# A hybrid decoder block: attention sinks as one more key column, and fewer vector operations around it

## The chip, the cores and the metric

The kernel runs on one core of a Trainium2 chip. The metric is device time in microseconds (us), from three runs: 1900.37, 1901.00 and 1901.44 us, median 1901.0. One execution was profiled as well. It took 1900.13 us, of which 1898.4 us lie between the first and the last instruction (the span).

The engines named below are PE (matrix products; PEld is its weight load), DVE (vector operations), ACT (activations and copies), POOL (masks and part of the DMA issues) and SP (the other DMA issues).

## The reference, cut to what matters

One layer over 2048 positions of width 1024, in float32: a normalized input is projected into a convolution branch, an attention branch and gates; both branches are gated, projected, merged and projected once more. The change lies in the attention, which has 16 query heads, 4 key heads, head size 64, blocks of 128 positions and a window of 128 keys. Each head has a learned sink, a score without a key: it takes part in the maximum and in the denominator, and in nothing else.

```python
qb = q.reshape(b, nb, BLOCK, N_KV_HEADS, g, HEAD_DIM)          # q, k are RMS-normalized per head
scores = jnp.einsum('bnqhgd,bnkhd->bnhgqk', qb, kb) * HEAD_DIM ** -0.5
scores = jnp.where(valid, scores, NEG_INF)                      # 0 <= q_pos - k_pos < 128
m = jnp.maximum(jnp.max(scores, axis=-1, keepdims=True), sink)
p = jnp.exp(scores - m)
p = p / (jnp.sum(p, axis=-1, keepdims=True) + jnp.exp(sink - m))
out = jnp.einsum('bnhgqk,bnkhd->bnqhgd', p, vb)
```

## The kernel before

**Products.** The sequence is worked in two tiles of 1024 positions. Every float32 operand is held as a high and a low part, and a product is done as high x high, low x high and high x low. A 1024-wide projection is cut into units of 256 output columns (`sunit`), and a unit is computed with seven block products instead of eight, in the manner of Strassen: products 1 and 2 use weight blocks as loaded, the others use sums of blocks. One product is 12 matmuls with 512 moving columns each. The units follow each other on PE without a break: keys, values, queries, convolution (`cv`, `b`), gates (`ga`, `gb`), `z`, `za`, then the output projections `yb`, `ya` and `o`.

**The clock of the program.** `run` counts products: each product is one tick. `put(n, f)` files a step for tick n, and the steps of a tick are written out after its product, in the order in which they were filed. Five engines get their instructions in this written order and each works its own queue strictly in order, so a step that must wait holds up all that stands behind it on its engine. `Woven` (`vec`) carries a list of small vector steps; each vector operation that goes through it takes one more step from that list along, and each tick ends with up to four of them.

**Weight sums.** For a unit, `sums` files four vector operations over the raw weights `raw[k, h]`, each 128x512: one addition, then `raw[0,0] = raw[0,1] - raw[0,0]`, then `raw[1,1] -= raw[0,0]` and `raw[1,0] -= raw[0,0]`. ACT then casts pairs of blocks to the high part, and DVE subtracts to get the low part.

**Attention.** It is woven between the products of `cv` to `z`: 32 blocks in each tile (4 key heads x 8 blocks), 64 in all, each with 4 query heads; `STEPS_0` and `STEPS_1` say at which tick a block's scores stand. The steps of a block whose scores stand at tick n are:

- n-5: load of the queries (`q2`), queries and keys (`kq`) and the keys' low parts (`kz`, two buffers `lows`);
- n: `att_scores`. Six matmuls on PE into one PSUM tile of two banks, of which there is a single buffer (`ps_s`, tile `s`): for each half h of the positions one matmul with the low parts of the keys (384 moving columns, for two heads c), then two with 192 columns (one for each head c). Each head has 256 columns in `s`, of which 192 are used. Then on DVE a masked copy, a maximum over 128 columns, and three operations on 128x4 values: the maximum times the query's scale `rq`, the smaller of its negative and minus the sink, and sink minus maximum;
- n+1: `att_exp`. On ACT one exponential of 128x4 for the sink, then for each head an exponential over 128 columns, which also gives the row sum;
- n+2: `att_norm` and `att_flip`. On DVE the row sum plus the sink's exponential, a reciprocal, the product with `p`, and a transposition;
- n+4 to n+15: two turns through memory, masks on POOL (`xh`, `yp`, `xl`), six matmuls with the values (`po`), and the sum into `o`.

`rq` holds the query scales of a head group, made on DVE well ahead of the first block that uses it.

## Time and profile before

| | before |
|---|---|
| median of 3 runs | 1901.0 us (1900.37 to 1901.44) |
| the profiled execution | 1900.13 us, span 1898.4 us |
| PE busy | 1888.9 us, 8670 matmuls |
| DVE busy | 1547.3 us, 2620 instructions |
| ACT busy | 986.6 us, 1967 instructions |
| POOL busy | 590.5 us |
| DVE busy between 1100 and 1150 us (attention stage) | 45.82 of 50 us |

Busy time is the time in which an engine has an instruction in work. The ends of matmuls are modelled and overlap, so whether PE stands still is read from the starts of its matmuls: a group of `x12` matmuls is one product, and its length divided by 12 is the spacing of the starts. In a line of the timeline, the numbers are start and duration in us; a bracket at the end names idle time before the instruction and what ended it.

### The profile page before, as it was taken

Reading aid. Unit: us, or ns where it says so; the run is one execution under the profiler, and the core shown is the slowest. Engines: PE = TensorE matmul, PEld = TensorE weight load, DVE = VectorE, ACT = ScalarE, POOL = GpSimd, SP = SyncE. Lnnn points to the kernel's source line nnn. Section 1 sums busy time; section 2 is a strip of 40 time slices with the busy share of each in tenths; the row PEclk is TensorE's granted clock in tenths of the full one; section 3 lists DMA queues with packets and bytes.
Section 4 is the critical chain, followed back from the end, with each engine's and each line's share of the span. In section 5 each row is a group of like instructions: output and inputs, shape, how many; then the busy total and the mean of one; then the engine's idle time right before and its main releaser. Section 6 shows DMA issues by size and latency. Waiting matters only on the chain.

```text
span 1898.4 us, 27426 instructions
## 1 busy us (share of the span) xinstructions
PE 1888.9 (100%) x8670; PEld 1572.3 (83%) x8670; DVE 1547.3 (82%) x2620; ACT 986.6 (52%) x1967; POOL 590.5 (31%) x846
## 2 busy tenths in 40 slices
PE   9999999999999999999999999999999999999999
PEld 7888888888888888888888888888888888888887
DVE  7988898898888767669799899888888777787754
ACT  7665455456666443434565545556666434444321
POOL 2073335335655000011462344445556000121000
PEclk9999999999999999999999999999999999999999
DMA  8286555558777857894584655567788887779653
GB/s 294 80 239 178 166 159 171 172 183 248 240 237 230 301 195 247 281 279 113 170 229 118 193 165 152 168 200 234 235 247 270 300 280 267 274 193 269 212 176 111
DMA packets 222497, 402.22 MB, mean 212 GB/s; under 512 B 30032, under 2 KB 104784, under 8 KB 212880
## 3 DMA queue, kind: packets, MB, share of 16 engines
q1 hardware_dynamic: 188224, 313.10, 50.4%
q0 software_dynamic: 30528, 78.94, 16.0%
q10 hardware_dynamic: 3600, 8.42, 1.3%
q8 instruction: 69, 1.13, 0.2%
q14 instruction: 76, 0.62, 0.1%
HBM read 271.09 MB, written 129.25 MB: 211 GB/s over the span
## 4 chain that ended last, share of the span: by engine, by line
PE 89%; DVE 5%; DMA 2%; ACT 2%; issue 1%; SPq 0%; POOL 0%; DVEq 0%; ACTq 0%; POOLq 0%
PE Y L640 33%; PE Xcv L640 4%; PE Vcv L640 4%; PE ya L1468 4%; PE Vq L640 2%; PE Xq L640 2%; PE Xyb L640 2%; PE Vyb L640 2%; PE Vo L640 2%; PE Xo L640 2%; PE Vza L640 2%; PE Xza L640 2%; PE po L1330 2%; PE Xgb L640 2%; PE Vgb L640 2%; PE Xga L640 2%
## 5 line engine op out<-in xcount | busy, mean ns | idle before, releaser
L1292 POOL DMA_DIRECT2D x<-fd x256 | 139.6, 552 | 128.8 <-DMA fd<-f 55.6
L1265 ACT ACTIVATE p<-s,st,rq 128x128 f32<-128x128 f32 x256 | 113.0, 450 | 0.1
L1313 POOL TENSOR_SCALAR_AFFINE_SELECT xh<-xh 64x512 fp32r<-64x512 f32 x64 | 59.3, 927 | 152.7 <-DVE xl L278 103.7
L1285 POOL DMA_DIRECT2D fd<-f x64 | 36.9, 577 | 209.4 <-DVE f L278 173.4
L1551 POOL DMA_DIRECT2D mt<-tha x16 | 13.8, 862 | 255.0 <-DVE tha L278 233.4
L640 PE MATMUL Xcv<-oph,wcv_ah 128*128 128x512 f32 x256 | 79.2, 390 | 0.0
L1313 POOL TENSOR_SCALAR_AFFINE_SELECT xl<-xl 64x512 fp32r<-64x512 f32 x64 | 66.2, 1034 | 4.4
L1313 POOL TENSOR_SCALAR_AFFINE_SELECT yp<-xl 64x512 fp32r<-64x512 f32 x64 | 58.2, 909 | 3.1
L1313 POOL TENSOR_SCALAR_AFFINE_SELECT yp<-yp 64x512 fp32r<-64x512 f32 x64 | 57.4, 898 | 4.2
L278 DVE SCALAR_TENSOR_TENSOR y<-u,cols,y 128x512 f32<-128x512 f32 x64 | 53.3, 834 | 3.8 <-ACT y L1379 2.7
L278 DVE TENSOR_TENSOR o<-po,o 64x256 f32<-64x256 f32 x128 | 53.4, 417 | 2.7 <-ACT o L1342 1.7
L640 PEld LDWEIGHTS Xcv<-oph,wcv_ah 128*128 128x128 f32 x256 | 47.6, 188 | 9.6
L278 DVE TENSOR_TENSOR p<-p,st 128x512 f32<-128x512 f32 x64 | 50.5, 790 | 3.3
L469 ACT CAST wcv_sh<-wcv_raw 128x1024 fp32r<-128x1024 f32 x16 | 16.8, 1051 | 69.7 <-DVE wcv_raw L278 69.7
L1265 ACT ACTIVATION_READ_ACCUMULATOR p<-s,st,rq 128x1 f32 x256 | 50.7, 198 | 0.0
L1342 ACT COPY o<-po 64x256 f32<-64x256 f32 x128 | 47.1, 368 | 6.2 <-DMA wpd_yb<-wph_yb 3.0
L1070 POOL DMA_DIRECT2D q2d<-q_h x64 | 44.2, 690 | 18.1 <-ACT q_h L1065 9.2
L640 PE MATMUL Xcv<-oph,wcv_al 128*128 128x512 f32 x128 | 49.8, 389 | 0.0
L2040 POOL DMA_DIRECT2D oc<-ocd x12 | 6.5, 543 | 136.0 <-DMA wyb_sh<-wpd_yb 119.7
L1070 POOL DMA_DIRECT2D q2d<-q_l x64 | 44.1, 689 | 13.7 <-DMA q2d<-q_h 5.0
L278 DVE TENSOR_TENSOR wcv_raw<-wcv_raw 128x512 f32<-128x512 f32 x64 | 47.3, 758 | 1.1
L278 DVE STREAM_TRANSPOSE f<-p 128x512 f32<-128x512 f32 x64 | 45.5, 711 | 2.9 <-DVE p L278 0.2
(713 smaller groups left out, 6457.9 us busy)
## 6 DMA issues: line engine op xcount, KB each, us to landing
gd<-th SPq DMA_DIRECT2D x64, 256.0 KB, 2.7
wcv_raw<-in_w_units SPq DMA_DIRECT2D x16, 1024.0 KB, 5.4
q<-q2d SPq DMA_DIRECT2D x64, 256.0 KB, 5.4
v<-vd SPq DMA_DIRECT2D x128, 128.0 KB, 3.5
fd<-f POOLq DMA_DIRECT2D x64, 256.0 KB, 4.4
x<-fd POOLq DMA_DIRECT2D x256, 64.0 KB, 3.2
th<-gd SPq DMA_DIRECT2D x48, 256.0 KB, 4.9
wga_raw<-in_w_units SPq DMA_DIRECT2D x8, 1024.0 KB, 5.3
```

Source lines behind the costliest of these rows:

```text
L278: r = f(*args, **kw)
L469: return (lambda: nc.scalar.copy(hi, src), lambda: vec.tensor_tensor(out=lo, in0=src, in1=hi.bitcast(F32), op=ALU.subtract))
L640: nc.tensor.matmul(ps, lhsT=w[:, j, :], rhs=b[:, m, :], start=start and j == 0 and i == 0, stop=j == KP - 1 and i == 2, skip_group_check=n ...
L1070: nc.gpsimd.dma_start(q2d[t][j][half, q * 2 * HB : (q + 1) * 2 * HB, i, e, :], src[HALVES[e]].bitcast(F32).rearrange("p (b x) -> p b x", x ...
L1265: nc.scalar.activation(out=p[:, i, :], in_=sg[:, i, HD : 3 * HD], func=AF.Exp, bias=st[:, 1, i : i + 1], scale=rv[:, i // 2, i % 2 : i % 2 ...
L1285: nc.gpsimd.dma_start(fd, f)
L1292: nc.gpsimd.dma_start(x[QUADS[k]], src[k])
L1313: nc.gpsimd.affine_select(out=d4, in_=s4, pattern=[[0, 2], [-32 * sg, 2], [0, G], [-sg, 32]], compare_op=ALU.is_gt if prev else ALU.is_ge, ...
L1330: nc.tensor.matmul(po[:, cs], lhsT=v2[:, kind + h, :], rhs=xx[:, :, h * HD : (h + 1) * HD], start=n == h == 0, stop=n == 2 and h == 1)
L1342: nc.scalar.copy(ov, pov[oth, :, e])
L1468: nc.tensor.matmul(ps, lhsT=w[:, j, cs], rhs=o[:, m, :], start=n == 0 and i == 0, stop=n == KC - 1 and i == 2)
L1551: nc.gpsimd.dma_start(mt[t][k, :, hs(q)], m, accum_op=ALU.add)
```

## The change

**The sink becomes a column.** For each head group, right after `rq` is made, DVE computes sink divided by `rq` for all its blocks (`keep_query`: a reciprocal and a product of 128x32, eight times in the kernel). Two ticks ahead of a block's scores a new step, `att_bank`, takes the tile `s` and has ACT copy the four quotients into column 192 of each head (128x4). Maximum, exponential and row sum then run over 129 columns instead of 128, so that the sink takes part in them. The 128x4 operations "times `rq`", "sink minus maximum" and "row sum plus sink" on DVE go, and so does the exponential of the sink on ACT. `p` has rows of 129 now, and the tiles of its pool are 2064 bytes long instead of 2048.

**Order of the score matmuls.** Within a half, the two matmuls of 192 columns come first, and the one of 384 columns comes last and adds to them.

**Weight sums.** The last two of the four subtractions in `sums` become one of 128x1024. `small` tiles have 10 buffers instead of 12, the tile `st` has 4 of its own.

```diff
+    def keep_query(t, j, rq):
+        rqs[t, j] = rq
+        sr = sinks_of[t, j] = consts.tile(
+            [P, 2, HB, 2, 2], F32, tag="sr_", bufs=4, name=f"sinks{t}_{j}")
+        s4 = sr.rearrange("p q b h c -> p (q b) (h c)")
+        vec.reciprocal(out=s4, in_=rq.rearrange("p q b h c -> p (q b) (h c)"))
+        mul(s4, s4, sink_r[:, j].rearrange("p h c -> p (h c)").unsqueeze(1).to_broadcast([P, NB, G]))
...
+    def att_bank(t, j, b):
+        sp = ps_s.tile([P, 2, 2, 2 * P], F32, tag="s", name=f"s{t}_{j}_{b}")
+        nc.scalar.copy(sp[:, :, :, 3 * HD : 3 * HD + 1], sinks_of[t, j][:, b // HB, b % HB].unsqueeze(3))
+        return sp
...
-            nc.tensor.matmul(
-                sp[:, h, :, skip : 3 * HD], lhsT=kq[:, 1, h * P : (h + 1) * P], rhs=kz[:, :, keys],
-                start=True, stop=False)
             for c in range(2):
                 nc.tensor.matmul(
                     sp[:, h, c, skip : 3 * HD], lhsT=q2[:, h, c, :], rhs=kq[:, 0, keys],
-                    start=False, stop=c == 1)
+                    start=c == 0, stop=False)
+            nc.tensor.matmul(
+                sp[:, h, :, skip : 3 * HD], lhsT=kq[:, 1, h * P : (h + 1) * P], rhs=kz[:, :, keys],
+                start=False, stop=True)
...
-        vec.tensor_reduce(out=st[:, 0], in_=sg[:, :, HD : 3 * HD], axis=AX.X, op=ALU.max)
-        mul(st[:, 5].rearrange("p (h c) -> p h c", c=2), st[:, 0].rearrange("p (h c) -> p h c", c=2), rv)
+        vec.tensor_reduce(out=st[:, 0], in_=sg[:, :, HD : 3 * HD + 1], axis=AX.X, op=ALU.max)
         vec.scalar_tensor_tensor(
-            out=st[:, 1], in0=st[:, 5], scalar=-1.0, in1=nsink_r[:, j].rearrange("p h c -> p (h c)"),
-            op0=ALU.mult, op1=ALU.min)
-        add(st[:, 2], sink_r[:, j].rearrange("p h c -> p (h c)"), st[:, 1])
+            out=st[:, 1], in0=st[:, 0], scalar=-1.0, in1=rv.rearrange("p h c -> p (h c)"),
+            op0=ALU.mult, op1=ALU.mult)
...
-        nc.scalar.activation(out=st[:, 3], in_=st[:, 2], func=AF.Exp)
-        p = slot([P, G, P], F32, f"p{t}_{j}_{b}")
+        p = slot([P, G, P + 1], F32, f"p{t}_{j}_{b}")
...
-        add(st[:, 5], st[:, 4], st[:, 3])
-        vec.reciprocal(out=st[:, 0], in_=st[:, 5])
+        vec.reciprocal(out=st[:, 0], in_=st[:, 2])
...
-                        lambda: sub(raw[:, 1, 1], raw[:, 1, 1], raw[:, 0, 0]),
-                        lambda: sub(raw[:, 1, 0], raw[:, 1, 0], raw[:, 0, 0])))
+                        lambda: sub(raw[:, 1].rearrange("p h j c -> p h (j c)"),
+                                    raw[:, 1].rearrange("p h j c -> p h (j c)"),
+                                    raw[:, 0, 0].rearrange("p j c -> p (j c)").unsqueeze(1).to_broadcast(
+                                        [P, 2, H]))))
...
+            put(n - 2, step("k", lambda g, j=j, b=b: att_bank(t, j, b)))
-            put(n, step("s", lambda g, j=j, b=b: att_scores(t, j, b, g["l"])))
+            put(n, step("s", lambda g, j=j, b=b: att_scores(t, j, b, g["l"], g["k"])))
```

What this does to the queues is shown at three places. In the names, `s_3_7` is the score tile of head group 3, block 7, the last of the first tile; `_1` after `wz` or `Xz` is the number of the unit; the last number counts tiles.

ACT, at the last block of the first tile, before: casts and copies of four blocks, three gates, and the copy `Y<-Xz` for which a later product of PE waits.

```order
L469 CAST wz_1_sh<-wz_1_raw 128x1024
L1342 COPY o_3_3_6174<-po_3_3_6136 64x4x2x32 x2
L1299 CAST xh_3_4_6177<-x_3_4_6002 128x512
L1300 CAST yp_3_4_6179<-x_3_4_6002 64x512
L1436 ACTIVATE zs_1_1_6134<-zs_1_1_6134 128x512
L1436 ACTIVATE zs_1_0_6195<-Y 128x512
L469 CAST wz_1_th<-wz_1_raw 128x1024
L658 COPY Y<-Xz_1_6229 128x512
```

The same place after:

```order
L466 CAST wz_1_sh<-wz_1_raw 128x1024
L1350 COPY o_3_3_6066<-po_3_3_6030 64x4x2x32 x2
L1307 CAST xh_3_4_6069<-x_3_4_5900 128x512
L1308 CAST yp_3_4_6071<-x_3_4_5900 64x512
L1237 COPY s_3_7_6074<-sinks_3_1925 128x4
L1444 ACTIVATE zs_1_1_6028<-zs_1_1_6028 128x512
L1444 ACTIVATE zs_1_0_6089<-Y 128x512
L466 CAST wz_1_th<-wz_1_raw 128x1024
L657 COPY Y<-Xz_1_6123 128x512
```

The sink copy of block 7 stands behind the two casts of an older block, `xh_3_4` and `yp_3_4`; the block's scores on PE now wait for it.

PE, the scores of the same block, before and after:

```order
L640 MATMUL Xz_1_6229<-oph_1_3_516,wz_1_al 128x512
L1236 MATMUL s_3_7_6245<-lows_148,kq_3_7_6049 128x2x192
L1240 MATMUL s_3_7_6245<-kq_3_7_6049,q_0_3_7_6047 128x192 x2
L1236 MATMUL s_3_7_6245<-lows_148,kq_3_7_6049 128x2x192
L1240 MATMUL s_3_7_6245<-kq_3_7_6049,q_0_3_7_6047 128x192 x2
L640 MATMUL Vz_1_6260<-oph_5_0_750,wz_1_sh 128x512 x2
```

```order
L639 MATMUL Xz_1_6123<-oph_1_3_514,wz_1_al 128x512
L1249 MATMUL s_3_7_6074<-kq_3_7_5947,q_0_3_7_5945 128x192 x2
L1252 MATMUL s_3_7_6074<-lows_147,kq_3_7_5947 128x2x192
L1249 MATMUL s_3_7_6074<-kq_3_7_5947,q_0_3_7_5945 128x192 x2
L1252 MATMUL s_3_7_6074<-lows_147,kq_3_7_5947 128x2x192
L639 MATMUL Vz_1_6151<-oph_5_0_747,wz_1_sh 128x512 x2
```

The same six matmuls in the same place, with each 384-column one (128x2x192) moved behind its two 192-column ones. On PE nothing else moves, and on POOL and SP nothing at all.

DVE, head group 0, block 4 of the second tile, from its mask to the weight sums of unit `b` 1, before (`vr` is the sum on which PE's next product waits, since it frees `Y`):

```order
L278 COPY_PREDICATED s_0_4_10726<-mask_i,s_0_4_10726 128x4x64
L278 TENSOR_REDUCE st_0_4_10734<-s_0_4_10726 128x4
L278 TENSOR_TENSOR st_0_4_10734<-st_0_4_10734,rq_0_9582 128x4
L278 SCALAR_TENSOR_TENSOR st_0_4_10734<-st_0_4_10734,nsink_r 128x4
L278 TENSOR_TENSOR st_0_4_10734<-cols,st_0_4_10734 128x4
...
L278 TENSOR_TENSOR st_0_4_10734<-st_0_4_10734 128x4
L278 RECIPROCAL st_0_4_10734<-st_0_4_10734 128x4
L278 TENSOR_TENSOR p_0_4_10780<-p_0_4_10780,st_0_4_10734 128x512
L278 STREAM_TRANSPOSE f_0_4_10805<-p_0_4_10780 128x512
L278 TENSOR_TENSOR wb_1_d<-wb_1_raw,wb_1_d 128x512
L278 TENSOR_TENSOR vr_3_10822<-Y,s5cv_3_10716 128x512
L278 TENSOR_TENSOR wb_1_raw<-wb_1_raw 128x512 x4
```

And after:

```order
L275 COPY_PREDICATED s_0_4_10542<-mask_i,s_0_4_10542 128x4x64
L275 TENSOR_REDUCE st_0_4_10606<-s_0_4_10542 128x4
L275 SCALAR_TENSOR_TENSOR st_0_4_10606<-st_0_4_10606,rq_0_9459 128x4
...
L275 RECIPROCAL st_0_4_10606<-st_0_4_10606 128x4
L275 TENSOR_TENSOR p_0_4_10649<-p_0_4_10649,st_0_4_10606 128x4x128
L275 STREAM_TRANSPOSE f_0_4_10673<-p_0_4_10649 128x512
L275 TENSOR_TENSOR wb_1_d<-wb_1_raw,wb_1_d 128x512
L275 TENSOR_TENSOR vr_3_10690<-Y,s5cv_3_10589 128x512
L275 TENSOR_TENSOR wb_1_raw<-wb_1_raw 128x512 x2
L275 TENSOR_TENSOR wb_1_raw<-wb_1_raw 128x1024
```

Three small operations less stand ahead of `vr`, and two of the four weight sums are one. Over the whole kernel DVE gets 256 instructions less (192 of 128x4, one more at the start, 79 in merged sums, and 16 more for the quotients).

More of the change, by code (lines that the diff above doesn't have):

```diff
@@ L149, in block_kernel @@
     upool = ctx.enter_context(tc.tile_pool(name="upool", bufs=2))
-    small = ctx.enter_context(tc.tile_pool(name="small", bufs=12))
+    small = ctx.enter_context(tc.tile_pool(name="small", bufs=10))
     ps_x = ctx.enter_context(tc.tile_pool(name="ps_x", bufs=2, space=bass.MemoryType.PSUM))
@@ L218, in block_kernel @@
     sink_r = cols[:, C_S:NC].rearrange("p (j h c) -> p j h c", h=2, c=2)
-    nsink_r = consts.tile([P, NKV, 2, 2], F32, name="nsink_r")
     gqk = consts.tile([P, 1], F32, name="gqk")
@@ L233, in prep_cols @@
             out=hbias, in0=cols[:, C_B:C_Q], scalar1=0.5, scalar2=None, op0=ALU.mult)
-        nc.vector.tensor_scalar(
-            out=nsink_r, in0=sink_r, scalar1=-1.0, scalar2=None, op0=ALU.mult)
     def tap(i, c):
@@ L1092, in by_query @@
                     vec.tensor_copy(rq[HALVES[e], :, :, h, :], rv[HALVES[h], :, :, :, e])
-            rqs[t, j] = rq
+            keep_query(t, j, rq)
         return fin
@@ L1231, in att_scores @@
         rv = rqs[t, j][:, b // HB, b % HB]
-        sp = ps_s.tile([P, 2, 2, 2 * P], F32, tag="s", name=f"s{nm}")
         for h in range(2):
@@ L1250, in att_scores @@
             vec.copy_predicated(sg[:, :, 2 * HD : 3 * HD], m, sg[:, :, 0:HD])
[L1251 to L1253 removed]
+        st = small.tile([P, 3, G], F32, tag="st", bufs=4, name=f"st{nm}")
+        vec.tensor_reduce(out=st[:, 0], in_=sg[:, :, HD : 3 * HD + 1], axis=AX.X, op=ALU.max)
         vec.scalar_tensor_tensor(
[L1255 to L1257 removed]
+            out=st[:, 1], in0=st[:, 0], scalar=-1.0, in1=rv.rearrange("p h c -> p (h c)"),
+            op0=ALU.mult, op1=ALU.mult)
         return sg, st, rv
```

13 lines of the change are left out of this document (6 added, 7 removed).

## The prediction

> **What bounds the kernel now.** I read the page first (busy shares, and the chain of work that ended last), then the chain in order of time, then PE's timeline, and last the groups of the tiles that the change touches.
>
> ```profile
> PE 1888.9 (100%) x8670; PEld 1572.3 (83%) x8670; DVE 1547.3 (82%) x2620; ACT 986.6 (52%) x1967; POOL 590.5 (31%) x846
> PE 89%; DVE 5%; DMA 2%; ACT 2%; issue 1%; SPq 0%; POOL 0%; DVEq 0%; ACTq 0%; POOLq 0%
> ...
> 151.01 2.72 PE Vq L640 x12
> 153.73 2.72 PE Y L640 x12
> ```
>
> PE is busy from end to end, and the chain runs through it for 89%. A busy PE need not be PE at its peak, so the second pair of lines matters more: one product follows the other every 2.72 us, 0.227 us for a matmul with 512 moving columns. No line of the change shortens that. DVE work that lies beside such products is hidden, whatever it costs. What DVE and ACT can give or take is only the places where a matmul starts later than 0.227 us after the one before. I went along PE's timeline for starts over 0.2 us late. Behind the opening and inside the stages with attention there are eight:
>
> ```profile
> 478.60 0.39 PE L640 MATMUL Vgb<-oph,wgb_sl 128*128 128x512 f32 x1
> 479.14 0.73 PE L640 MATMUL Y<-oph,wgb_sh 128*128 128x512 f32 x2
> ...
> 589.96 0.39 PE L640 MATMUL Vz<-oph,wz_sl 128*128 128x512 f32 x1
> 590.46 0.73 PE L640 MATMUL Y<-oph,wz_sh 128*128 128x512 f32 x2
> ...
> 1100.67 0.40 PE L1330 MATMUL po<-yp,v 128*128 128x256 f32 x2
> 1100.91 0.40 PE L1330 MATMUL po<-xl,v 128*128 128x256 f32 x2
> 1101.48 0.72 PE L640 MATMUL Y<-oph,wcv_d 128*128 128x512 f32 x2 [0.17 <-DVE vr L278]
> ...
> 1115.86 0.39 PE L640 MATMUL Xb<-oph,wb_al 128*128 128x512 f32 x1
> 1116.65 0.73 PE L640 MATMUL Y<-oph,wb_th 128*128 128x512 f32 x2 [0.40 <-DVE Vb L278]
> ...
> 1165.58 0.40 PE L1330 MATMUL po<-xl,v 128*128 128x256 f32 x2
> 1166.19 0.73 PE L640 MATMUL Y<-oph,wcv_d 128*128 128x512 f32 x2 [0.21 <-DVE vr L278]
> ...
> 1196.49 0.39 PE L640 MATMUL Vcv<-oph,wcv_sl 128*128 128x512 f32 x1
> 1196.93 0.73 PE L640 MATMUL Y<-oph,wcv_sh 128*128 128x512 f32 x2
> ...
> 1459.34 0.50 PE L1330 MATMUL po<-xl,v 128*128 128x256 f32 x2 [0.87 <-POOL xl L1313]
> 1510.55 0.73 PE L640 MATMUL Y<-oph,wz_d 128*128 128x512 f32 x2 [0.24 <-DVE zs L278]
> ```
>
> The first pair: 478.60 + 0.227 = 478.83, and the next matmul starts at 479.14, 0.31 late. Its group of two lasts 0.73 instead of 0.227 + 0.39 = 0.62, so a stop costs another 0.11 behind it. In the same way the stops cost 0.31 + 0.11 = 0.42 us at 479, 0.27 + 0.11 = 0.38 at 590, 0.33 + 0.11 = 0.44 at 1101 (two `po` matmuls take 0.24, from the starts 1100.67 and 1100.91), 0.56 + 0.11 = 0.67 at 1117, 0.37 + 0.11 = 0.48 at 1166 and 0.21 + 0.11 = 0.32 at 1197. The last two wait for masks on POOL and for a sum behind loads, where the change takes nothing away.
>
> **Part 1: the small operations that go.**
>
> ```profile
> L278 DVE TENSOR_TENSOR st<-st,rq x64: 153/163/631, 183.2 to 1439.4; 128x4 f32<-128x4 f32 x64
> L278 DVE SCALAR_TENSOR_TENSOR st<-st,nsink_r x64: 154/162/712, 183.4 to 1439.6; 128x4 f32<-128x4 f32 x64
> L278 DVE TENSOR_TENSOR st<-cols,st x64: 154/163/600, 183.6 to 1439.8; 128x4 f32<-128x4 f32 x64
> L1262 ACT ACTIVATE st<-st x64: 196/206/209, 183.8 to 1440.3; 128x4 f32<-128x4 f32 x64
> L278 DVE TENSOR_TENSOR st<-st x64: 148/162/673, 188.3 to 1444.3; 128x4 f32<-128x4 f32 x64
> ```
>
> For each block the first, the third and the last of these go, 0.16 us each by the median, and the second takes another operand. DVE gets 64 x 0.48 = 31 us shorter. The longest cases, 0.60 to 0.67 us, are an operation of the same size held up by something else, and I take it that the next one is then held up in its place. ACT loses 0.21 us ahead of the four exponentials and gets a copy of 128x4 at another place, for which the nearest row is the exponential that goes: 0.21 us. One column more in 128 is within 1% of the maximum and of the exponentials; eight pairs of 128x32 operations come ahead of the blocks, in a stretch in which no product waits.
>
> All this lies beside products, except ahead of five of the stops. At 479 and at 1197 the matmul waits for ACT's copy `Y`, which stands behind four exponentials; they start earlier by the 0.16 us of the sum in the normalization before and by the 0.21 us of the sink's exponential, 0.37 us, which is more than the 0.31 and the 0.21 that are missing. At 1101 and at 1166 the sum `vr` stands on DVE behind mask, maximum, and normalization of one block: three operations less, 0.48 us, against 0.33 and 0.37. All four stops go: 0.42 + 0.32 + 0.44 + 0.48 = 1.66 us. At 1117 the sum `Vb` stands behind exponentials and normalization: 0.37 of 0.56 us, and the stop remains with 0.19 + 0.11. Together 2.03 us. What is late next at these places is `Y` itself, which the product before delivers.
>
> **Part 2: the sink copy two products ahead.** It stands in ACT's queue behind what was filed earlier for the same tick, and PE's score matmuls now wait for it. Behind the copy itself on ACT are the casts and gates of that tick, 0.21 us later, as they are earlier by the exponential that went: nothing. I went through all 64 places: what stands ahead of the copy ended, before the change, over 0.6 us ahead of the scores at 62 of them. The two others:
>
> ```profile
> 345.31 0.62 ACT L1300 CAST yp<-x 64x512 fp32r<-64x512 f32 x1
> 346.16 0.33 PE L1236 MATMUL s<-lows,kq 128*128 128x384 f32 x1
> ...
> 587.23 0.62 ACT L1300 CAST yp<-x 64x512 fp32r<-64x512 f32 x1
> 586.61 0.33 PE L1236 MATMUL s<-lows,kq 128*128 128x384 f32 x1
> ...
> L1240 PEldq EVENT_SEMAPHORE  x64: 51/51/51, 176.9 to 1436.3; - x64
> ```
>
> At 346 the cast ends at 345.93; with 0.48 us off DVE ahead of it and 0.21 us for the copy, the bank is ready at 345.66, in time. At 586, the last block of the first tile, the cast ends at 587.85, 1.24 us after the scores began. It moves forward by 0.37 (the exponentials there start behind a table load, so that only one sum and the sink's exponential help), the copy adds 0.21: ready at 587.69, and PE stands for 1.08 + 0.11 us. Then come the waits of the low-part matmul, which now stand in the middle of the block: three instructions of 0.051 us that PE's sequencer passed unseen so far, since it runs ahead. Between 0 and 0.15 us; after a stop it has no lead, so I take 0.15. Sum 1.34 us. In exchange the stop at 590 goes, since ACT's `Y` is then done while PE still works the product in between: -0.38. Net +0.96 us.
>
> **Part 3: the order of the score matmuls.**
>
> ```profile
> 285.51 0.33 PE L1236 MATMUL s<-lows,kq 128*128 128x384 f32 x1
> 285.69 0.36 PE L1240 MATMUL s<-kq,q 128*128 128x192 f32 x2
> 285.88 0.36 PE L1236 MATMUL s<-lows,kq 128*128 128x384 f32 x1
> 286.08 0.36 PE L1240 MATMUL s<-kq,q 128*128 128x192 f32 x2
> 286.28 0.42 PE L640 MATMUL Y<-oph,wcv_sh 128*128 128x512 f32 x1
> ```
>
> The same six matmuls with the same widths. The 384-column one takes 0.18 us behind a product and 0.20 behind a 192-column one. Afterwards both stand behind a 192-column one, and the product behind a wide one instead of a narrow one. A cost of 0.03 us a block and a gain of the same size are equally near: +-1.9 us for 64 blocks, and I take 0.
>
> **Part 4: two subtractions as one.**
>
> ```profile
> 65.94 0.68 DVE L278 TENSOR_TENSOR wq_raw<-wq_raw 128x512 f32<-128x512 f32 x1
> 66.55 0.68 DVE L278 TENSOR_TENSOR oph<-xt,oph 128x512 fp32r<-128x512 f32 x1
> 67.15 0.68 DVE L278 TENSOR_TENSOR wq_raw<-wq_raw 128x512 f32<-128x512 f32 x1
> ...
> 1107.98 1.22 DVE L278 TENSOR_TENSOR wb_tl<-wb_raw,wb_th 128x1024 fp32r<-128x1024 f32 x1
> 1109.11 0.41 DVE L278 TENSOR_TENSOR o<-po,o 64x256 f32<-64x256 f32 x1
> ...
> 68.48 0.51 PE L755 MATMUL Qga<-oph,wga_p0h 128*128 128x512 f32 x1 [0.23 <-DVE oph L278]
> ```
>
> Two operations of 128x512 that don't wait for each other start 0.60 us apart, 1.21 for two; one of 128x1024 takes 1.13 until the next starts. 79 x 0.08 = 6 us off DVE, hidden beside products. In the opening, where the two stood apart, the merged one holds the operand `oph` at 66.55 back by 0.53 us and lets the following one go 0.08 us earlier. PE waits for both, and the second wait, which ends at 68.48, then falls into the first: net 0, at most +0.4. [...]
>
> **Sum.** -2.03 + 0.96 + 0 + 0 = -1.07 us. The profiled execution took 1900.13, so 1899.1 for one like it; the median of the runs lies 0.9 above that execution, which gives 1899.9 us.
>
> **Rivals.**
>
> *Faster by more than 0.2%.* About 0.2%, 3.8 us here, is what a measurement of this kernel can tell from no change. If the copy at 586 comes in time after all, all six stops go: 0.42 + 0.38 + 0.44 + 0.67 + 0.48 + 0.32 = 2.7 us, and with 0.03 us saved in each score block 4.6 us: 1896.4. Against it: the cast at 586 is 1.24 us late, and nothing that goes is that long.
>
> [...]
>
> *The gains drown.* Where small operations are long, something else holds DVE, and an operation less gains nothing; then the stops stay and only the +0.96 comes: 1902.0. For it speak the 0.6 us cases in the rows above.
>
> *Slower by more than 0.2%.* The sink copy is late at other blocks too. A late one costs about 1.3 us, so from four more on (+0.96 - 2.03 + 4 x 1.3 = +4.1 us, 1905.1) it decides. Against it: 62 places with over 0.6 us, and an ACT queue that gets earlier. It would take ACT work that waits for something which the change delays.
>
> **How the numbers follow.** My sum, anything from -3 to 0 us: 0.50. The gains drown or a little more is lost, 0 to +3.8 us: 0.25. Faster than 0.2%: 0.15, of which 0.02 for headroom on PE. Slower: 0.10. So faster 0.15, same 0.75, slower 0.10. The range takes the best rival's 1896.4 nearly in (1896.8) and on the other side the drowned gains with the bad end of the score order, 1902.0 + 1.9, cut to 1903.6. The likeliest case alone lies in 1898 to 1901.
>
> **What the profile after would show.** Right: no late start at the matmuls that answer to 479, 1101, 1166 and 1197; a wait of PE for ACT of over 1 us at the last score block of the first tile; score blocks as long as before; about 256 DVE instructions less with DVE busy near 1510 us, and PE busy unchanged. Wrong, if the spacing of matmuls inside or right behind score blocks changes, if PE waits for the copy at several blocks, or if new stops for DVE appear where merged sums stand.

## The result, and the profile after

The changed kernel takes 1903.73 us (median of 22 runs, 1900.12 to 1906.69); the kernel before took 1900.99 (median of 22 runs beside them). The ratio is 1.0014, 95% interval 1.0007 to 1.002: slower by 0.14%, or 2.7 us. The forecast was 1899.9 us, 1.1 faster, with a range from 1896.8 to 1903.6.

The profiled execution of the changed kernel took 1905.33 us, 5.2 more than that of before. The busy line of its page:

```profile
PE 1890.5 (99%) x8670; PEld 1574.2 (83%) x8670; DVE 1498.9 (79%) x2364; ACT 990.3 (52%) x1967; POOL 608.3 (32%) x846
```

DVE has 48 us and 256 instructions less, as it should. PE is still the bound. One number is odd: POOL is busy 608.3 us, 18 more than before, with the same 846 instructions, none of which the change touched.

Where the time went is seen from the starts of some score blocks on PE's timeline in the two profiled executions (us):

| score block | before | after | difference |
|---|---|---|---|
| first of tile 0 | 180.77 | 179.86 | -0.9 |
| 29th of tile 0 | 551.91 | 551.84 | -0.1 |
| last of tile 0 | 586.61 | 593.97 | +7.4 |
| first of tile 1 | 1032.13 | 1041.04 | +8.9 |
| last of tile 1 | 1437.22 | 1443.40 | +6.2 |

The change gains at the start, and from the first to the last block of tile 1. It loses 7.4 us within 42 us of tile 0. PE's timeline there:

```profile
575.28 0.39 PE L639 MATMUL Xz<-oph,wz_al 128*128 128x512 f32 x1
579.73 1.22 PE L639 MATMUL Y<-oph,wz_th 128*128 128x512 f32 x2 [4.05 <-DVE Vz L275]
...
581.17 1.05 PE L639 MATMUL Y<-oph,wz_th 128*128 128x512 f32 x2
```

```profile
576.00:578.00 2.00, 0.00 (x0) 1.00 0.82 212
...
580.00:582.00 2.00, 2.00 (x5) 0.50 0.15 45
```

The second fence is PE by stretches of 2 us: after the length stand busy time, matmuls, granted clock, DMA share and GB/s. The matmul that should start at 575.51 starts at 579.73, 4.2 us late, since it waits for the sum `Vz` on DVE. Behind it a dozen matmuls start 0.43 us apart instead of 0.227: the granted clock is 0.50. That is another 2.6 us. Another 0.5 us had gone at 568.85, where a matmul waits for a mask by POOL that came late (step 2 below).

The rest of the account is smaller. This execution also lost 1.8 us at 384 to 386, for masks by POOL, and 1.3 us at 645 and 651, for sums by DVE. In a second profile of the same kernel (below) only 0.4 us of these came, so they vary from execution to execution; the stop near 579 is in both.

The next views follow the wait back. First DVE, POOL and SP (its issues are named SPq) of the changed kernel, mixed in order of time, then DVE alone behind them:

```profile
563.33 0.68 DVE L275 TENSOR_TENSOR xl<-x,xh 128x512 fp32r<-128x512 f32 x1
563.93 0.17 DVE L275 RECIPROCAL st<-st 128x4 f32<-128x4 f32 x1
564.13 0.69 DVE L275 TENSOR_TENSOR p<-p,st 128x512 f32<-128x512 f32 x1
564.14 1.31 POOL L1321 TENSOR_SCALAR_AFFINE_SELECT xh<-xh 64x512 fp32r<-64x512 f32 x1 [3.76 <-DVE st L275]
...
566.96 1.22 DVE L275 TENSOR_TENSOR wz_tl<-wz_raw,wz_th 128x1024 fp32r<-128x1024 f32 x1
567.10 1.69 POOL L1321 TENSOR_SCALAR_AFFINE_SELECT xl<-xl 64x512 fp32r<-64x512 f32 x1
...
568.20 0.33 SPq L437 DMA_DIRECT2D wz_raw<-in_w_units  x1
568.76 0.58 POOL L1293 DMA_DIRECT2D fd<-f  x1
```

```profile
576.52 0.69 DVE L275 TENSOR_TENSOR xl<-x,xh 128x512 fp32r<-128x512 f32 x1 [7.58 <-issue]
...
578.97 0.70 DVE L275 TENSOR_TENSOR Vz<-s5z,Y 128x512 f32<-128x512 f32 x1
```

Last the issue of `fd` (size, and us from issue to landing) in the list of DMA issues, of the changed kernel and, in the fence behind it, of the kernel before:

```profile
fd<-f POOLq DMA_DIRECT2D x1, 256.0 KB, 7.7
```

```profile
fd<-f POOLq DMA_DIRECT2D x1, 256.0 KB, 4.6
```

The same work before the change:

```profile
561.74 0.69 DVE L278 TENSOR_TENSOR xl<-x,xh 128x512 fp32r<-128x512 f32 x1
562.34 0.16 DVE L278 TENSOR_TENSOR st<-st 128x4 f32<-128x4 f32 x1
...
562.56 0.76 POOL L1313 TENSOR_SCALAR_AFFINE_SELECT xh<-xh 64x512 fp32r<-64x512 f32 x1 [3.64 <-DVE st L278]
...
562.74 1.10 DVE L278 TENSOR_TENSOR p<-p,st 128x512 f32<-128x512 f32 x1
...
565.30 0.76 POOL L1313 TENSOR_SCALAR_AFFINE_SELECT xl<-xl 64x512 fp32r<-64x512 f32 x1
...
566.02 0.58 POOL L1285 DMA_DIRECT2D fd<-f  x1
...
566.37 1.22 DVE L278 TENSOR_TENSOR wz_tl<-wz_raw,wz_th 128x1024 fp32r<-128x1024 f32 x1
...
567.62 0.33 SPq L440 DMA_DIRECT2D wz_raw<-in_w_units  x1
```

Four steps are to be read from these rows.

1. Before, the scaling of `p` starts 1.00 us behind the subtraction `xl`, and POOL's first select 0.82 behind it. The select is first and takes 0.76; `p`, which is late, takes 1.10 instead of 0.69. After, the sum ahead of the reciprocal is gone (it took 0.20 with its start): `p` starts 0.80 us behind `xl`, the select 0.81, and now `p` is first and the select takes 1.31. The one that starts second stands until the first has ended: `p` ends at 564.82 and the select 0.63 later, though alone it takes 0.76.
2. The same happens at the last select. After, the weight difference `wz_tl` starts at 566.96, 0.14 ahead of it, because DVE lost neither 0.41 us at `p` nor the two small operations of the scores. The select takes 1.69 us instead of 0.76. So the store `fd` leaves 5.43 us behind `xl` instead of 4.28.
3. The end of `wz_tl` frees the buffer for the next weight load of 1 MB. Before, `fd` was issued 1.60 us ahead of that load; after, 0.56 behind it. It landed 4.6 us after its issue before, and 7.7 after.
4. The next `xl` on DVE waits for that landing: by the program's waits it needs the semaphore of this store, as it gets a buffer out of the rotating 19. The profile names no releaser for it (`issue` in the bracket), but DVE's wait for this semaphore ends at 576.48 in the trace, 0.04 behind the landing at 576.44, and `xl` starts at 576.52, with everything else in DVE's queue behind it, `Vz` too.

### The profile page after: what moved, and what is told of

Its sections match the earlier page's. It is cut to its first block, busy times and chain, and to the rows that moved or that the text cites. A ratio compares the mean times of both kernels' runs of the same rounds, so it can differ in the third digit from the quotient of the medians.

```text
span 1903.6 us, 27277 instructions
## 1 busy us (share of the span) xinstructions
PE 1890.5 (99%) x8670; PEld 1574.2 (83%) x8670; DVE 1498.9 (79%) x2364; ACT 990.3 (52%) x1967; POOL 608.3 (32%) x846
## 4 chain that ended last, share of the span: by engine, by line
PE 67%; DMA 1%; DVE 1%; issue 0%; SPq 0%; ACT 0%; DVEq 0%
PE Y L639 25%; PE ya L1476 4%; PE Vcv L639 2%; PE Xyb L639 2%; PE Xcv L639 2%; PE Vo L639 2%; PE Xo L639 2%; PE Vyb L639 2%; PE Vza L639 2%; PE Xza L639 2%; PE Vz L639 2%; PE Xz L639 2%; PE po L1338 1%; PE Vga L639 1%; PE Xgb L639 1%; PE Vgb L639 1%
## 5 line engine op out<-in xcount | busy, mean ns | idle before, releaser
L1274 ACT ACTIVATE p<-s,st,rq 128x129 f32<-128x129 f32 x256 | 114.2, 458 | 32.7 <-DVE st L275 22.9
L1321 POOL TENSOR_SCALAR_AFFINE_SELECT yp<-xl 64x512 fp32r<-64x512 f32 x64 | 70.2, 1097 | 3.1
L275 DVE TENSOR_TENSOR xl<-x,xh 128x512 fp32r<-128x512 f32 x64 | 43.7, 683 | 8.9 <-issue 8.1
L1249 PEld LDWEIGHTS s<-kq,q 128*128 128x128 f32 x256 | 46.1, 189 | 4.1 <-ACT s L1237 0.2
```

The source lines that it names most:

```text
L275: r = f(*args, **kw)
L1249: nc.tensor.matmul(sp[:, h, c, skip : 3 * HD], lhsT=q2[:, h, c, :], rhs=kq[:, 0, keys], start=c == 0, stop=False)
L1274: nc.scalar.activation(out=p[:, i, :], in_=sg[:, i, HD : 3 * HD + 1], func=AF.Exp, bias=st[:, 1, i : i + 1], scale=rv[:, i // 2, i % 2 : i ...
L1321: nc.gpsimd.affine_select(out=d4, in_=s4, pattern=[[0, 2], [-32 * sg, 2], [0, G], [-sg, 32]], compare_op=ALU.is_gt if prev else ALU.is_ge, ...
```

## The experiments

All ratios are to the kernel before on the same chip, with 95% intervals; they are worked out from all executions and can differ from the ratio of the two medians by up to 0.0005. The kernel before has a median of 1900.48 us beside the four runs of the first part, 1900.71 beside the second profile, the one sum more, the one operation less and the one load behind in the changed kernel, and 1901.0 beside the other four.

### Parts of the change alone

**The two subtractions apart again, all else as after.**

```diff
-lambda: sub(raw[:, 1].rearrange("p h j c -> p h (j c)"), ..., raw[:, 0, 0]... .to_broadcast([P, 2, H]))
+lambda: sub(raw[:, 1, 1], raw[:, 1, 1], raw[:, 0, 0]),
+lambda: sub(raw[:, 1, 0], raw[:, 1, 0], raw[:, 0, 0])
```

> The kernel after with the two subtractions apart again (part 4 undone), 6 us of VectorE work back. Theory A (the sink column takes 31 us off VectorE, weight loads of 1 MB go out earlier than the small transfers of the attention blocks, which then land late; the merged sums matter little): 2 to 3 us over the kernel before, as the changed kernel, with the stops near 385, 579 and 645. Rival B (the merged subtraction holds VectorE when a product waits for a sum): the 2.7 us go, within 0.6 us of the kernel before. Rival C (the order of the score matmuls or the early sink copy costs PE time inside the blocks): 2.7 us over, but without the stops.

Measured 1902.6 us (1899.87 to 1906.27), ratio 1.0009 (1.0 to 1.0018). The stop was there, 3.68 us at 577.5, without a drop of the clock behind it. So the merged sums are not its cause. Of the stops that were also expected near 385 and 645 its profiled execution (1899.87) shows none.

**The merged sums alone, in the kernel before.**

```diff
-lambda: sub(raw[:, 1, 1], raw[:, 1, 1], raw[:, 0, 0]),
-lambda: sub(raw[:, 1, 0], raw[:, 1, 0], raw[:, 0, 0])
+lambda: sub(raw[:, 1].rearrange("p h j c -> p h (j c)"), ..., raw[:, 0, 0]... .to_broadcast([P, 2, H]))
```

> The kernel before with the two subtractions as one and nothing else (part 4 alone). Theory A: within 1 us of the kernel before, the opening at 68 up to 0.5 us shorter, no stop of several us. Rival B: 2 to 3 us slower, with stops for sums by VectorE near 579 and 645. My recorded price for this part was 0.

Measured 1900.58 us (1899.1 to 1907.17), ratio 1.0005 (0.9997 to 1.0014): no change that can be told. `Vz` came 1.28 us late at 577, with `fd` ahead of the weight load; no stop of several us. POOL was busy 600.5 us instead of 590.5. PE's longest step in the opening, where the merged operation stands ahead of the operand `oph`:

```profile
66.66 0.40 PE L757 MATMUL Qga<-oph,wga_p0h 128*128 128x512 f32 x1
67.83 0.50 PE L757 MATMUL Qga<-oph,wga_p0h 128*128 128x512 f32 x1 [0.77 <-DVE oph L278]
```

Here the step is 1.17 us long; in the kernel before the longest was 0.62 (from 67.86 to 68.48), at the next `oph`. That is no loss of 0.55 us: PE came to this place 0.54 us earlier than in the kernel before, waited at one `oph` for long and not at the other, and left the place 0.03 later (69.09 against 69.06), as the last `oph` ended at 68.37 instead of 68.43. In the changed kernel the wait that ended at 68.48 is gone, since DVE gets there earlier (that `oph` ends at 67.52).

**The score order alone, in the kernel before.**

```diff
-matmul(sp[:, h, :, ...], lhsT=kq[:, 1, ...], rhs=kz[...], start=True, stop=False)
 for c in range(2):
-    matmul(sp[:, h, c, ...], lhsT=q2[:, h, c, :], rhs=kq[:, 0, keys], start=False, stop=c == 1)
+    matmul(sp[:, h, c, ...], lhsT=q2[:, h, c, :], rhs=kq[:, 0, keys], start=c == 0, stop=False)
+matmul(sp[:, h, :, ...], lhsT=kq[:, 1, ...], rhs=kz[...], start=False, stop=True)
```

> The kernel before with the six score matmuls in the new order and nothing else (part 3 alone). The trace after shows 12 matmul starts from the first score matmul on take 2.167 us in the mean, where before they took 2.179: 64 x 0.012 = 0.8 us shorter. So A and B: 0 to 1 us faster than the kernel before. Rival C: 2 to 3 us slower.

Measured 1901.4 us (1898.59 to 1906.63), ratio 1.0002 (0.9993 to 1.0011). No loss by the order can be told; a gain of 0.8 us cannot be told from none. In the median block twelve starts took 2.187 us here, 2.188 in the kernel before and 2.176 in the changed one, so the 0.8 us that were expected do not come from the order alone. Its profiled execution took 1906.63 and had the long stop at another place: 2.3 us at 387 for a select, and the half clock behind it (0.50 from 389 to 391). So single executions of a kernel close to the old one stop too, at a place that the change leaves as it is: at 370 `fd` stands 0.57 us behind a 1 MB load, `wga_raw`, in this run and 0.56 in the kernel before. The load took 9.2 us in that execution and 5.3 in the one of before.

**The small operations back, with no use.**

```diff
+mul(st[:, 3], st[:, 0], rv)          # before the two-operand product of the scores
+add(st[:, 4], st[:, 3], st[:, 1])    # behind it
+add(st[:, 5], st[:, 2], st[:, 4])    # before the reciprocal
```

> The kernel after with three small 128x4 operations on VectorE put back in each block, at the places of the three that went (their results are not used): 31 us of VectorE work back, all else as after. Theory A: VectorE's queue runs as late as before, the 1 MB loads go out as late as before, and the time falls to within 0.8 us of the kernel before, without the long stop near 579. Rivals B and C: stays 2.7 us over. A further rival D (the stops are a matter of chance in each execution and any change of timing moves them about): anywhere, with the spread of single executions as wide as after, 6 us, and stops at other places.

Measured 1899.21 us (1898.23 to 1903.2), ratio 0.9997 (0.9988 to 1.0006). With 192 useless operations the changed kernel goes from 2.7 us over the kernel before to 1.3 under it, and the stop near 579 is away (its profiled execution, of 1902.76 us, stopped for 2.0 us at 387 instead). So the shorter DVE work brought the stop, but the run leaves open whether the whole 31 us or one place matters.

### The place

**The changed kernel once more, for a second profile.** (No edit.)

> The changed kernel once more, for a second profile of it and its time on the chip that the three others run on. Theory E, formed from the first traces: in the normalization of block 28 of the first tile one small VectorE sum is gone, so the scaling of p starts 0.80 us behind the subtraction xl instead of 1.00, while GpSimd's first select starts 0.82 behind it; the two don't run beside each other, VectorE now comes first, GpSimd's four selects end over 1 us later, the store fd of f leaves 0.6 us behind the 1 MB weight load instead of 1.6 us ahead of it, lands 3 us or more later, and PE stands for the sum Vz. By E the stop of over 3 us near 579 is there again, and the time is 2 to 4 us over the kernel before. Rival D (chance in each execution): the stop is elsewhere or smaller.

Measured 1903.28 us (1901.89 to 1906.33), ratio 1.0012 (1.0003 to 1.0021). The stop is there again: 3.6 us late at 577.81, a dozen matmuls at half clock behind it. `p` started at 561.24, the select at 561.25; the load went at 565.30, `fd` at 565.87, and it took 8.7 us. Chance in each execution is out as the cause of this stop.

**One sum of 128x4 more, in one block.**

```diff
 def att_norm(got, one=False):
     p, st = got
+    if one:                                   # block 28 of the first tile
+        add(extra, st[:, 2], st[:, 1])
     vec.reciprocal(out=st[:, 0], in_=st[:, 2])
```

> The changed kernel with one VectorE sum of 128x4 added, in front of the reciprocal of block 28 of the first tile and nowhere else (its result isn't used). Theory E: the scaling starts at least 0.06 us behind GpSimd's first select, which then goes first; the selects take 0.76, 1.07, 0.73 and 0.76 us, fd is issued ahead of the weight load, the stop near 579 goes, and the time falls by 3 to 6 us against the changed kernel, to 1898.5 to 1900.5, at or under the kernel before. Theory A in its general form (31 us of VectorE work in all blocks) and rival D: no change against the changed kernel.

DVE, POOL and SP of this run at the place, in order of time:

```profile
559.62 0.68 DVE L275 TENSOR_TENSOR xl<-x,xh 128x512 fp32r<-128x512 f32 x1
560.22 0.16 DVE L275 TENSOR_TENSOR extra<-st 128x4 f32<-128x4 f32 x1
...
560.43 0.76 POOL L1324 TENSOR_SCALAR_AFFINE_SELECT xh<-xh 64x512 fp32r<-64x512 f32 x1 [3.16 <-DVE xl L275]
560.50 1.23 DVE L275 TENSOR_TENSOR p<-p,st 128x512 f32<-128x512 f32 x1
...
563.90 0.58 POOL L1296 DMA_DIRECT2D fd<-f  x1
...
565.09 0.33 SPq L437 DMA_DIRECT2D wz_raw<-in_w_units  x1
```

Measured 1898.66 us (1895.3 to 1901.99), ratio 0.9988 (0.9979 to 0.9996). One instruction of 0.16 us, whose result nobody reads, takes about 4.6 us off the changed kernel and puts it ahead of the kernel before. `p` starts 0.07 us behind the select, the four selects take the times that they had before (0.76, 1.06, 0.73 and 0.76), `fd` leaves 1.19 us ahead of the load, and no matmul waits near 573.

**One operation less, in the kernel before.**

```diff
-add(st[:, 5], st[:, 4], st[:, 3])
-vec.reciprocal(out=st[:, 0], in_=st[:, 5])
+add(st[:, 0], st[:, 4], st[:, 3])             # block 28 of the first tile alone
```

The kernel leaves out the reciprocal in that one block, where `p` is scaled by the sum itself, so the result of that block is not the reference's.

> The kernel before with one VectorE operation of 128x4 less, at the same place of the same block: the reciprocal is left out, so p of that one block is scaled by the sum itself. Theory E: the scaling starts 0.80 us behind xl, the first select 0.82; VectorE goes first, fd falls behind the weight load, PE stands near 577, 2 to 6 us slower than the kernel before. Since the margin is 0.02 us, E also holds if GpSimd still goes first and the time then doesn't move; it falls if VectorE goes first and no stop comes. Theory A in its general form and rival D: as the kernel before, within 0.8 us.

Measured 1900.26 us (1899.67 to 1901.77), ratio 0.9998 (0.9989 to 1.0007): nothing. The theory was half right. `p` came first as expected (562.98 against 563.01; the select took 1.29). But at the second meeting the last select was first, as DVE, POOL and SP of this run show:

```profile
565.95 0.76 POOL L1316 TENSOR_SCALAR_AFFINE_SELECT xl<-xl 64x512 fp32r<-64x512 f32 x1
566.11 0.60 DVE L278 TENSOR_TENSOR st<-cols,st 128x4 f32<-128x4 f32 x1
566.63 1.21 DVE L278 TENSOR_TENSOR wz_tl<-wz_raw,wz_th 128x1024 fp32r<-128x1024 f32 x1
566.67 0.58 POOL L1288 DMA_DIRECT2D fd<-f  x1
...
567.87 0.33 SPq L440 DMA_DIRECT2D wz_raw<-in_w_units  x1
```

The two small operations of the scores, which the change removes too, still stand ahead of `wz_tl`. So one missing operation is not enough, and the next run takes all three away.

**Three operations less, in the kernel before.** As above, and in block 29:

```diff
-mul(st[:, 5], st[:, 0], rv)
-vec.scalar_tensor_tensor(out=st[:, 1], in0=st[:, 5], scalar=-1.0, in1=nsink_r[:, j], op0=mult, op1=min)
-add(st[:, 2], sink_r[:, j], st[:, 1])
+vec.scalar_tensor_tensor(out=st[:, 1], in0=st[:, 0], scalar=-1.0, in1=rv, op0=mult, op1=mult)
-activation(out=st[:, 3], in_=st[:, 2], func=Exp)
+activation(out=st[:, 3], in_=st[:, 1], func=Exp, scale=0.0)   # the sink's exponential, of a constant
```

The kernel leaves out the reciprocal in block 28, and in block 29 the sink in the maximum; the sink's exponential there is that of a constant. So the result of these two blocks is not the reference's.

> The kernel before with three small VectorE operations less, all around one place: the reciprocal of block 28 of the first tile (p is scaled by the sum itself), and in block 29 the product with the norms and the sum with the sinks (that block's maximum leaves the sink out, and its sink's exponential is taken of a constant). With one operation less VectorE got the first collision (scaling against first select) but not the second: the last select started at 565.95, and the difference wz_tl 0.68 later. Theory E: with the two others gone wz_tl starts about 0.15 us ahead of the last select, which then ends after it; fd is issued 0.6 us behind the weight load, and PE stands 3 to 4.5 us for Vz near 578, with some matmuls at half the clock behind it in part of the executions: 3 to 6 us slower than the kernel before. If E is wrong: within 0.8 us of the kernel before.

DVE, POOL and SP of this run, and behind them PE's stop from its timeline:

```profile
562.33 0.69 DVE L278 TENSOR_TENSOR p<-p,st 128x512 f32<-128x512 f32 x1
562.35 1.29 POOL L1321 TENSOR_SCALAR_AFFINE_SELECT xh<-xh 64x512 fp32r<-64x512 f32 x1 [3.63 <-DVE st L278]
...
565.15 1.21 DVE L278 TENSOR_TENSOR wz_tl<-wz_raw,wz_th 128x1024 fp32r<-128x1024 f32 x1
565.29 1.69 POOL L1321 TENSOR_SCALAR_AFFINE_SELECT xl<-xl 64x512 fp32r<-64x512 f32 x1
...
566.39 0.33 SPq L440 DMA_DIRECT2D wz_raw<-in_w_units  x1
566.95 0.58 POOL L1293 DMA_DIRECT2D fd<-f  x1
```

```profile
578.71 0.73 PE L640 MATMUL Y<-oph,wz_th 128*128 128x512 f32 x2 [4.21 <-DVE Vz L278]
```

Measured 1905.68 us (1905.15 to 1907.98), ratio 1.0025 (1.0015 to 1.0035). Three small operations less on DVE, without the sink column, the new order or the merged sums, make the kernel before 4.7 us slower, with the same 0.14 us at the last select, the same 0.56 us behind the load, and the same stop. This is the stop of the changed kernel, made without the rest of the change.

### The load

**That one load behind three small transfers of its tick, in the changed kernel.**

```diff
-ahead_loads()
+if tick[0] != 186: ahead_loads()
 ...                                           # the work filed for the tick
+if tick[0] == 186: ahead_loads()
```

> The changed kernel with that one 1 MB load (wz_raw at 568) issued behind the three small transfers of its tick on SyncE's queue, about 2 to 3 us later, and all engines' own orders as they are. Theory E with the load as the cause: the selects on GpSimd end as late as in the changed kernel (fd issued 5.4 us behind xl), but fd then is ahead of the load and lands in 3 to 5 us instead of 7.7, the stop near 579 shrinks from 4.2 us to under 1, and the time falls by 2 to 5 us. If the late selects alone are the cause, the stop stays over 3 us.

POOL and SP of this run:

```profile
567.97 1.69 POOL L1324 TENSOR_SCALAR_AFFINE_SELECT xl<-xl 64x512 fp32r<-64x512 f32 x1
...
569.63 0.58 POOL L1296 DMA_DIRECT2D fd<-f  x1
...
571.50 0.56 SPq L437 DMA_DIRECT2D wz_raw<-in_w_units  x1
```

Measured 1899.04 us (1897.04 to 1901.43), ratio 0.9988 (0.9979 to 0.9997). The selects are as late as in the changed kernel, but `fd` is ahead of the load, lands after 3.4 us, and the stop is gone. The late selects alone don't cost the time; the place of `fd` behind the load does.

**The same load behind, in the kernel before.** (The same edit.)

> The kernel before with the one weight load at 568 behind the three small transfers of its tick, as in the run on the changed kernel that took 4 us off. Theory E (in the kernel before fd is ahead of that load anyway): nothing, within 0.8 us of the kernel before. If moving this load is a gain of its own, whatever the sink column does: 2 to 4 us faster.

Measured 1900.19 us (1899.61 to 1901.09), ratio 0.9995 (0.9986 to 1.0004). No gain of its own: what the edit gave in the changed kernel is what the change had lost there.

**All loads from tick 60 on behind.**

```diff
-ahead_loads()
+if tick[0] < 60: ahead_loads()
 ...
+if tick[0] >= 60: ahead_loads()
```

> The changed kernel with every 1 MB weight load from tick 60 on issued behind the small transfers of its tick instead of ahead of them. If what helped at 568 is a general rule (a large load ahead of a small transfer that is waited for), the chance stops near 385 get rarer too: 1898 to 1899.5, and a narrower spread. Against it: small loads of queries, keys and values that now go ahead of the weight load wait for their own buffers, and hold the weight load back on the same queue; a sum or cast of weights then comes late: over 1902.

Measured 1899.94 us (1898.5 to 1903.71), ratio 0.9994 (0.9985 to 1.0003). The run does not test what it was meant to. At the end of a tick buffers count as free that did not at its start, so the loads moved one tick forward, and the end of one tick adjoins the start of the next: in SP's order only two loads moved, ahead of the four transfers `zin` beside them. `fd` was 0.56 us behind its load again (568.31 against 567.75) and took 6.5 us instead of 7.7, as the load took 5.4; the stop was 2.9 us. In its profiled execution the stop was 1.3 us shorter than in that of the changed kernel and there was no half clock behind it (2.6 us there), which would cover the 3 us and more by which this kernel lies under the changed one. Why the clock did not fall stays open.

Taken together, the fourteen profiled executions agree: in the five with `fd` 0.56 us behind this load (the changed kernel twice, the subtractions apart, the three operations less, this run) PE stopped for 2.9 to 4.4 us near 577, and in the nine with `fd` ahead of it for 1.3 at most.

### The change without the stop and without the merged sums

**The one sum more, and the two subtractions apart.** (Both edits shown above.)

> The changed kernel with the one sum more in block 28 and with the two subtractions apart again: the sink column and the score order, without part 4 and without the stop near 579. Against the kernel with the one sum and the merged subtraction (0.9988 of before) it shows what part 4 is worth when that stop is away. By my prediction 0: 0.9985 to 0.9992. If the merged form holds VectorE somewhere, faster than that; if the shorter VectorE helps, slower, up to 1.000.

Measured 1896.92 us (1896.17 to 1898.32), ratio 0.9978 (0.9968 to 0.9988): the fastest of all, 4.1 us under the kernel before. In its profiled execution only two matmuls behind the first score block are over 0.15 us late, at 878 and at 1456. PE's timeline where the kernel before stopped at 479:

```profile
477.48 0.39 PE L637 MATMUL Vgb<-oph,wgb_sl 128*128 128x512 f32 x1
477.73 0.73 PE L637 MATMUL Y<-oph,wgb_sh 128*128 128x512 f32 x2
```

Of the 0.31 us there 0.02 are left (477.73 against 477.48 + 0.227).

Against the same kernel with merged sums (1898.66, on another chip) it is 1.7 us faster by the medians; the two intervals overlap, and the profiled executions differ by 0.1 us (1896.51 and 1896.60). So that the merged sums cost a little is likely (all three pairs point that way) and not shown.

## Why the prediction was wrong, and where it was right

**The bound: right.** PE stays the bound, 1890.5 us busy, one product per 2.72 us. DVE ended at 1498.9 us (near 1510 was forecast) with 256 instructions less. By the busy times of the runs the merge alone took 9.3 us off (1538.0 with it; 6 was forecast), and the changed kernel without the merge was 39.5 us shorter (1507.8; 31 was forecast). No run shows the headroom on PE for which 0.02 of the chance of "faster" was counted: with 48 us less on DVE the products still follow each other every 2.72 us.

**Part 1, the stops: right in sign and size, and wrong in the sentence on the rest of the kernel.** The stops at 1101, 1166 and 1197 are gone. That at 479 fell from 0.42 to 0.15 us, and that at 1117 to 0.17, where 0.30 was expected:

```profile
1124.03 0.39 PE L639 MATMUL Xb<-oph,wb_al 128*128 128x512 f32 x1
1124.32 0.73 PE L639 MATMUL Y<-oph,wb_th 128*128 128x512 f32 x2
```

The failed step is the sentence "All this lies beside products, except ahead of five of the stops." It costed 31 us less DVE work as free wherever no product waited, and asked only which waits get shorter. It did not ask what DVE, being earlier, would start ahead of. At one place of the kernel, around block 28 of the first tile, that was a select of POOL, twice, and through the freed buffer a load on SP's queue ahead of a store on POOL's. What the prediction put at nothing there was a stop of 4.2 us, with 2.6 us more at half clock behind it. The rows to see it stand in the trace of before: select 0.18 us ahead of `p`, and 0.20 us of DVE work about to go from in front of `p`; `fd` 1.60 us ahead of a 1 MB load.

**Part 2, the sink copy: wrong by its whole size.** The +1.34 us did not come, and the stop at 590 went all the same. In the changed kernel the copy ends just in time, 0.115 us before the block's first matmul:

```profile
593.04 0.62 ACT L1308 CAST yp<-x 64x512 fp32r<-64x512 f32 x1
593.69 0.17 ACT L1237 COPY s<-sinks 128x4 f32<-128x4 f32 x1
```

The cast ahead of it ended 1.24 us behind the start of the block before, and now 0.31 ahead of it. The prediction moved it by 0.37. The missing term is a wait ahead of it on ACT, which was in the trace and was not looked at:

```profile
584.73 1.05 ACT L469 CAST wz_sh<-wz_raw 128x1024 fp32r<-128x1024 f32 x1 [1.42 <-DVE wz_raw L278]
```

ACT stood 1.42 us for DVE's weight sums there; with DVE earlier, it doesn't. The 0.37 us of the exponentials, on the other hand, could not come through here: behind them ACT waits for PE's product `Vz` (0.51 us before the change, 1.92 in the last run). In all eight profiled executions with the new copy it ended 0.05 to 0.12 us before that block: it is the one place of 64 with next to no margin, but not late.

**Part 3, the score order: right within its bounds.** Twelve starts from the first score matmul on take 2.167 us in the mean, where they took 2.179. Times 64 that is 0.8 us shorter; 0 with +-1.9 was taken. The order alone did not bring it (2.187 us in the median block, as before); what did is not shown.

**Part 4, the merged sums: right that DVE's saving is hidden.** The prediction's net 0 in the opening held: with the merge alone PE left that place 0.03 us later than in the kernel before. A loss of the 0.53 us by which the merged form holds `oph` back is not seen in these runs. What the part missed: the merged operation holds a select of POOL longer than either of the two did. In the changed kernel the select that starts inside it at 318.54 takes 1.61 us; in the kernel before those that start inside the two, at 319.78 and 320.93, take 1.08 each. POOL's busy time rose by 10 us with the merge alone and by 7 with the rest of the change alone (597.9 us).

**The sum and the rivals.** Without the stop the forecast gain would have been too small: 1.1 us, where the kernel with the one sum more gained 2. The rival "faster" named the case that the last run shows: the copy in time, all six stops gone, 1896.4; measured 1896.9 with the merged sums apart. That the number is so near is in part luck: the rival counted 0.03 us saved in each score block, and 0.012 came. "Slower" had the right direction by the wrong mechanism: no sink copy was late anywhere. "The gains drown" had 1902.0, near the result, but no gain drowned; one new wait of 4 us plus the half clock behind it outweighed them.

## What to carry to other kernels

An engine with slack that gets shorter is not free: list what it will start ahead of, operations on another engine that stand when both run (here a select took 1.31 or 1.69 us instead of 0.76), and transfers that its end releases. Where two of those lie within a few tenths of a us in the trace, the order can be decided by next to nothing, and a small operation more or less can turn it; here 0.16 us decided over 4.6. A large load issued just ahead of a small transfer that someone waits for was the dangerous case here (`fd` landed after 7.7 us instead of 4.6), and moving the load behind it was the cure that doesn't rest on which of two operations starts first.

## What the runs showed of the hardware

**DVE's sums, differences and scaling and POOL's selects excluded each other here.** A select of 0.76 us took 1.31 behind `p`, and 1.69 behind `wz_tl`: in the changed kernel `wz_tl` ends at 568.18 and the select at 568.79, 0.61 later. All four long selects in the rows of the changed kernel and of the three operations less end 0.61 to 0.63 us behind the operation on DVE, whenever they were issued. The other way round `p` took 1.10 or 1.23 instead of 0.69. Transpose, mask and maximum between them lengthened no select: before the change those at 564.49 and 565.30, beside the end of the transpose, the mask and the maximum, took 0.73 and 0.76 us. The order of the starts decided which one stood, down to 0.01 us of difference: in the changed kernel `p` started at 564.13 and the select at 564.14, and the select took 1.31. What makes the two engines exclude each other, no run shows.

**The small transfer waited for the large one ahead of it, though on another queue.** The DMA records of the traces show `fd` as 64 pieces of 4 KB and the load as 128 of 8 KB. In the four kernels with the stop, and in a second profile of one of them, `fd` was issued 0.56 us behind the load; its first piece started 3.9 to 4.6 us after the issue, when 79 to 108 of the load's 128 had started, and in the run with all loads behind when all 128 had. Outside that run the last pieces of both ended within 0.2 us of each other. Ahead of the load (in the nine other profiles) the first piece of `fd` started 1.2 to 1.9 us after the issue. So the two did not share the engines evenly; what decides their shares is not shown.

**The half clock did not follow the length of the pause.** PE's clock fell to 0.50 behind a pause of 1.37 us in one run (the load behind, at 387), and stayed at 1.00 behind one of 3.52 (the subtractions apart, at 577):

```profile
386.64 0.50 PE L1341 MATMUL po<-xl,v 128*128 128x256 f32 x2 [1.37 <-POOL xl L1324]
...
388.52 0.63 PE L639 MATMUL Xb<-oph,wb_al 128*128 128x512 f32 x1
```

```profile
577.50 0.72 PE L637 MATMUL Y<-oph,wz_th 128*128 128x512 f32 x2 [3.52 <-DVE Vz L275]
578.06 0.40 PE L637 MATMUL Y<-oph,wz_tl 128*128 128x512 f32 x1
```

In the first fence, of the one run, a matmul behind the pause takes 0.63 us, at half the clock (0.50 from 388 to 390); in the second, of the other, it takes 0.40, at the full one (1.00 from 578 to 580).

In the clock records the stretch at half clock behind the 1.37 us lasts 3.41 us, and that behind the stop of the changed kernel 6.83, twice as long. What decides whether the clock falls, and for how long, stays open. With the fall or without it, similar stops cost 7 us in one execution and 4 in another.
